# The compute engines of a two-layer transformer trunk, ordered by another scheduler model

## Chip, cores, metric

One core of one Trainium2 chip. The metric is device microseconds of one launch, the median of several runs.

## What is computed

Two layers over 512 tokens of width 1024: 256 context tokens, which read only each other, and 256 latent tokens, which read all. Each layer takes one normalised and modulated input through three token mixers (latent attention, "MLA"; differential attention; windowed attention with a sink), merges them with gates, projects, and then runs a SwiGLU feed-forward. A small product with `w_ada` gives each layer its shifts, scales and gates.

```python
def merge_branches(o_a, o_b, o_c, gates, wa, wb, wc, wo):
    ga, gb, gc = jnp.split(gates, N_BRANCH, axis=-1)
    return (ga * (o_a @ wa) + gb * (o_b @ wb) + gc * (o_c @ wc)) @ wo
...
def swiglu(h, w_gate_up, w_down):
    g, u = jnp.split(h @ w_gate_up, 2, axis=-1)
    return (jax.nn.silu(g) * u) @ w_down
...
def adaln(cond, w, b):
    return jnp.split(jax.nn.silu(cond) @ w + b, 6, axis=-1)
```

## The kernel before

**Tiling.** The tokens stand in four tiles of 128. Every product of two matrices is made in three passes on numbers that are split into a high and a low part (`mm3`, L267, L268, L269: high by high, high by low, low by high). A weight block is loaded by SyncE into one of three `raw` buffers (`do_load`, L166); ScalarE casts the high part into one of three `hl` buffers (L139) and VectorE subtracts to get the low part (L140). The load of a later block can go out only when a `raw` buffer has been split.

**Attention** runs as steps S, E, T, V (`attend`). S is a product into `psS` (L721, L791). E finds the row maximum on VectorE (L663, with L665 and, for the window, a floor), takes the exponential on ScalarE (L667), and for every second step a reciprocal (L739, L800) and the scaling of the weights on VectorE (L745; L801, L803, L804 for the differential mixer). T transposes the weights on TensorE (L673), V multiplies by the values (L758). There are two `psS` buffers, so an S waits for the L667 of two steps earlier. L1059 and L1036 copy queries and values of the MLA into place; L823 sums squares of the differential output; L382 and L383 finish a gate.

**The ada stream** (`ada_dve`) is spread through the other work of a layer: two `aw` buffers, loaded by SyncE (L350), are multiplied and summed on VectorE by L401 and L403 (16 instructions for each half of a quarter), then TensorE sums over the partitions (L361), ScalarE copies (L363), TensorE transposes (L367). A gate goes by another way: its row is written to memory (L372) and read back to all partitions into `gw` (L380), L376 and L377 load what L382 and L383 add and multiply.

**Between the sub-layers** `normed` (L431 to L436), `modulate_T` (transposes L442; L455 on VectorE for one half and L457 on ScalarE for the other; L459 and L460 split the result into `hT`) and `residual` (sum of squares L298, L475, L477 and L479 on GpSimd, L482) make the next input from the last product.

**The order.** TensorE and SyncE run in the order in which the program is written, since the trunk declares these two engines to be ordered by hand:

```python
    ctx.enter_context(tc.manual_schedule(engines={mybir.EngineType.PE, mybir.EngineType.SP}))
```

The program interleaves attention steps, blocks of weights and the ada stream by a table of costs (`drive`, `fillers`, `attend`). The queues of VectorE, ScalarE and GpSimd are ordered at compile time by the scheduler of the tile framework, from the same program, by a model of when each instruction can run. Each engine then runs its queue in that order, and where the head of a queue waits, all behind it wait as well.

## Time and profile before

| | |
|---|---|
| median of 3 runs | 1530.48 us (1529.92 to 1534.97) |
| profiled execution | 1534.5 us |
| its span | 1532.7 us |
| TensorE, matmuls, busy | 1464.7 us, 96% |
| TensorE, weight loads, busy | 1228.9 us, 80% |
| VectorE busy | 1028.6 us, 67% |
| ScalarE busy | 690.0 us, 45% |
| GpSimd busy | 155.8 us, 10% |
| mean granted clock of TensorE | 0.986 |

The profiled execution took 4.0 us more than the median of the three. A share of busy time is a mean over stages; where TensorE waits and for whom is to be seen in the waits and on the time line. On this time line layer 0 has its MLA from 103 to 225 us, the differential mixer to 345, the window mixer to 482, the merge and output projection to 620, gate-up with the ada stream to 860, down to 985. Layer 1 has its mixers to 1260, the output projection to 1340, gate-up to 1466, and ends at 1532.

### The profile page before, as it was taken

To read this page: it belongs to the slowest core of one execution; us is meant where nothing else is said; L and a number is where in the kernel's file an instruction comes from. 1 tells how busy PE (TensorE), PEld (TensorE's weight loads), DVE (VectorE), ACT (ScalarE), POOL (GpSimd) and SP (SyncE) were. 2 spreads that over 40 slices of the span, in tenths; PEclk is the share of its full clock that TensorE was granted. 3 is DMA by queue.
4 is the path that set the end of the run, shared out by engine and by line. 5 is a ranking of instruction groups with operands and counts; after the bars stand their busy time and mean duration, and the time that the engine had idled before them with its cause. 6 is when DMAs were issued, how large, how long until landed. Compare 5 with 4: busy or idle time off the path is not lost. (4 is left out here: it accounts for less than half of the span.)

```text
span 1532.7 us, 23209 instructions
## 1 busy us (share of the span) xinstructions
PE 1464.7 (96%) x8827; PEld 1228.9 (80%) x8827; DVE 1028.6 (67%) x2035; ACT 690.0 (45%) x1293; POOL 155.8 (10%) x217
## 2 busy tenths in 40 slices
PE   6989999998999999999999999998999999999998
PEld 5866677876777879887777788886898899799986
DVE  4678766887885554687877323578677776666654
ACT  4565554444554345332232213565555564544443
POOL 1222100022110001000000000133101300100000
PEclk9989999999999999999999999999999999999999
DMA  9532223434332452566567334424436436667664
GB/s 288 154 106 69 69 83 97 110 84 137 95 98 72 144 170 83 163 194 176 168 192 219 110 97 128 148 79 135 108 93 155 130 99 190 195 194 218 207 219 166
DMA packets 254243, 216.25 MB, mean 141 GB/s; under 512 B 24426, under 2 KB 236084, under 8 KB 254132
## 3 DMA queue, kind: packets, MB, share of 16 engines
q1 hardware_dynamic: 252464, 209.98, 47.0%
q10 hardware_dynamic: 1668, 4.80, 0.8%
q8 instruction: 69, 1.13, 0.3%
q14 instruction: 42, 0.34, 0.1%
HBM read 209.48 MB, written 5.27 MB: 140 GB/s over the span
## 5 line engine op out<-in xcount | busy, mean ns | idle before, releaser
L267 PE MATMUL psg<-hT,hl 128*128 128x256 f32 (+1 forms) x1328 | 478.2, 360 | 0.0
L268 PE MATMUL psg<-hT,hl 128*128 128x256 f32 (+1 forms) x1328 | 451.4, 340 | 0.3 <-DVE hT L460 0.3
L269 PE MATMUL psg<-hT,hl 128*128 128x256 f32 (+1 forms) x1328 | 451.3, 340 | 0.1
L140 DVE TENSOR_TENSOR hl<-raw,hl 128x1024 fp32r<-128x1024 f32 (+2 forms) x243 | 293.4, 1209 | 201.0 <-ACT hl L139 200.1
L139 ACT CAST hl<-raw 128x1024 fp32r<-128x1024 f32 (+2 forms) x243 | 243.6, 1004 | 318.8 <-PE psg L269 185.7
L267 PEld LDWEIGHTS psg<-hT,hl 128*128 128x128 f32 x1328 | 254.2, 191 | 37.8 <-issue 14.4
L269 PEld LDWEIGHTS psg<-hT,hl 128*128 128x128 f32 x1328 | 253.7, 191 | 28.9 <-DVE hl L140 0.3
L268 PEld LDWEIGHTS psg<-hT,hl 128*128 128x128 f32 x1328 | 254.8, 192 | 25.3 <-issue 4.2
L403 DVE SCALAR_TENSOR_TENSOR acc<-aw,siluc,acc 128x256 f32<-128x256 f32 x448 | 201.7, 485 | 14.0 <-DMA aw<-in_w_ada 11.4
L667 ACT ACTIVATE work<-psS,nm 128x512 f32<-128x512 f32 (+1 forms) x96 | 59.1, 616 | 51.9 <-DVE nm L665 47.6
L477 POOL TENSOR_SCALAR smy<-ssy 128x1 f32<-128x1 f32 x12 | 4.1, 339 | 725.8 <-ACT work L298 725.8
L673 PE MATMUL psT<-ca,work 128*128 128x128 f32 x400 | 65.1, 278 | 8.3 <-DVE work L804 3.8
L663 DVE TENSOR_REDUCE nm<-psS 128x1 f32<-128x512 f32 (+1 forms) x96 | 57.1, 595 | 18.7 <-PE psS L721 11.4
L267 PE MATMUL psg<-oT,hl 128*128 128x512 f32 (+1 forms) x192 | 69.5, 362 | 0.0
L673 PEld LDWEIGHTS psT<-ca,work 128*128 128x128 f32 x400 | 48.6, 143 | 21.6 <-issue 8.5
L269 PE MATMUL psg<-oT,hl 128*128 128x512 f32 (+1 forms) x192 | 64.8, 338 | 0.2 <-DVE hl L140 0.2
L268 PE MATMUL psg<-oT,hl 128*128 128x512 f32 (+1 forms) x192 | 64.7, 337 | 0.0
L676 ACT COPY work<-psT 128x512 f32<-128x512 f32 (+1 forms) x72 | 36.8, 511 | 54.5 <-PE psT L673 54.2
L267 PE MATMUL psg<-hl,hT 128*128 128x256 f32 (+1 forms) x168 | 57.8, 344 | 2.7 <-ACT hT L139 2.7
L721 PE MATMUL psS<-kT,qT 96*128 96x512 f32 (+1 forms) x96 | 45.6, 560 | 10.6 <-ACT work L667 10.6
L269 PE MATMUL psg<-hl,hT 128*128 128x256 f32 (+1 forms) x168 | 48.1, 286 | 0.8 <-DVE hT L140 0.8
L268 PE MATMUL psg<-hl,hT 128*128 128x256 f32 (+1 forms) x168 | 47.7, 284 | 0.0
(325 smaller groups left out, 2572.2 us busy)
## 6 DMA issues: line engine op xcount, KB each, us to landing
raw<-in_w_gate_up SPq DMA_DIRECT2D x88, 512.0 KB
aw<-in_w_ada SPq DMA_DIRECT2D x80, 512.0 KB
raw<-in_w_in SPq DMA_DIRECT2D x78, 512.0 KB
raw<-in_w_down SPq DMA_DIRECT2D x44, 512.0 KB
aw<-in_w_ada SPq DMA_DIRECT2D x32, 256.0 KB
raw<-in_w_o SPq DMA_DIRECT2D x16, 512.0 KB
raw<-in_w_branch_a SPq DMA_DIRECT2D x8, 512.0 KB
raw<-in_w_in SPq DMA_DIRECT2D x16, 256.0 KB
```

The lines of the kernel that those rows point to most:

```text
L139: nc.scalar.copy(hi, src)
L140: nc.vector.tensor_tensor(lo, src, hi.bitcast(F32), ALU.subtract)
L267: nc.tensor.matmul(ps, lhsT=asl(a[0], k), rhs=bsl(b[0], k), start=st, stop=False)
L268: nc.tensor.matmul(ps, lhsT=asl(a[0], k), rhs=bsl(b[1], k), start=False, stop=False)
L269: nc.tensor.matmul(ps, lhsT=asl(a[1], k), rhs=bsl(b[0], k), start=False, stop=en)
L403: nc.vector.scalar_tensor_tensor(acc[:, s], w[:, k], sc, acc[:, s], ALU.mult, ALU.add)
L477: nc.gpsimd.tensor_scalar(sm, ss[:, 0:1], ss[:, 1:2], D * EPS, ALU.add, ALU.add)
L663: nc.vector.tensor_reduce(nm, ps[:, :nk], AX.X, ALU.max, negate=True)
L667: nc.scalar.activation(st["p"][:, :nk], ps[:, :nk], AF.Exp, bias=nm, accum_out=sm)
L673: nc.tensor.transpose(pt[:, k * P:(k + 1) * P], st["p"][:, k * P:(k + 1) * P], ident)
L676: nc.scalar.copy(st["pT"][:, :nk], pt[:, :nk])
L721: nc.tensor.matmul(st["ps"][:, :nk], lhsT=q, rhs=k, start=z == 0, stop=z == len(ops) - 1 and mk is None)
```

## The change

The context that holds the program gets one argument more, by which the compile-time scheduler uses its time-line model instead of its default model.

```diff
-    with tile.TileContext(nc) as tc:
+    with tile.TileContext(nc, schedule_with_timeline_sim=True) as tc:
         trunk(tc, *args)
```

Instructions are the same in number and kind. The queues of TensorE and SyncE are the same row by row, 7178 and 314 rows. VectorE's queue reads 1566 rows in place of 1555, ScalarE's 919 in place of 927; GpSimd's keeps its 198 rows, some in another order. 864 tiles lie in another buffer of their pool. In the MLA stage, the first L663 and L665 that stood behind four L1059 copies stand ahead of them; at about 169 us an L665 stands ahead of an L143 and of the L955 and L956 of a stack of operands, behind which it stood; and at about 123 us two L401 and two L403 stand ahead of an L745 where one L403 stood. In the window mixer, at about 413 us, six L403, one L663 and one split L140 stand between two L401 and an L745 that stood right behind them. Three other places, shown below:

VectorE, differential mixer of layer 0 (about 250 us), up to the scaled weights of one step, L804, for which its transposes wait. `hl` and `raw` are a weight block, `aw`, `siluc` and `acc` the ada stream, `nmd`, `sm` and `rsd` maximum, sum and reciprocal of the softmax. Before, from the reciprocal L800 on:

```order
L800 RECIPROCAL rsd<-sm_2613 128x2
L663 TENSOR_REDUCE nmd<-psS 128x1
L140 TENSOR_TENSOR hl<-raw,hl 128x1024
L801 TENSOR_TENSOR rsd<-rsd,lam 128x1
L403 SCALAR_TENSOR_TENSOR acc<-aw,siluc,acc 128x256
L803 TENSOR_SCALAR work<-work,rsd 128x256
L403 SCALAR_TENSOR_TENSOR acc<-aw,siluc,acc 128x256
L804 SCALAR_TENSOR_TENSOR work<-work,rsd 128x256
```

and after, from one L403 ahead of it:

```order
L403 SCALAR_TENSOR_TENSOR acc<-aw,siluc,acc 128x256
L800 RECIPROCAL rsd<-sm_2613 128x2
L403 SCALAR_TENSOR_TENSOR acc<-aw,siluc,acc 128x256
L663 TENSOR_REDUCE nmd<-psS 128x1
L140 TENSOR_TENSOR hl<-raw,hl 128x1024
L403 SCALAR_TENSOR_TENSOR acc<-aw,siluc,acc 128x256
L801 TENSOR_TENSOR rsd<-rsd,lam 128x1
L403 SCALAR_TENSOR_TENSOR acc<-aw,siluc,acc 128x256 x2
L803 TENSOR_SCALAR work<-work,rsd 128x256
L823 TENSOR_REDUCE ssd<-work 128x4
L663 TENSOR_REDUCE nmd<-psS 128x1
L804 SCALAR_TENSOR_TENSOR work<-work,rsd 128x256
```

Five L403 in place of two, the sum of squares L823 and one more maximum L663 now stand ahead of L804; just ahead of this piece three L403 stand in place of two.

VectorE, gate-up of layer 0 (about 662 us). `gw` is the gate that a DMA brings back, `raw` the weight block to split. Before:

```order
L140 TENSOR_TENSOR hl<-raw,hl 128x1024
L140 TENSOR_TENSOR aT<-work,aT 128x512
L403 SCALAR_TENSOR_TENSOR acc<-aw,siluc,acc 128x256
L140 TENSOR_TENSOR hl<-raw,hl 128x1024
L382 TENSOR_TENSOR gw<-gw,work 128x256 x2
L383 SCALAR_TENSOR_TENSOR gw<-gw,work 128x256 x2
L401 TENSOR_SCALAR acc<-aw,siluc 128x256 x2
```

and after:

```order
L403 SCALAR_TENSOR_TENSOR acc<-aw,siluc,acc 128x256
L140 TENSOR_TENSOR hl<-raw,hl 128x1024
L140 TENSOR_TENSOR aT<-work,aT 128x512
L382 TENSOR_TENSOR gw<-gw,work 128x256 x2
L140 TENSOR_TENSOR hl<-raw,hl 128x1024
L383 SCALAR_TENSOR_TENSOR gw<-gw,work 128x256 x2
L401 TENSOR_SCALAR acc<-aw,siluc 128x256 x2
```

The second split of a weight block (L140 `hl`) has moved behind the two L382, which read `gw`.

ScalarE, end of layer 0 (about 985 us), where the last tiles are normalised and the first weights of layer 1 are cast:

```order
+L139 CAST hl<-raw 128x1024
 L436 ACTIVATE work<-xt,rn 128x512
-L457 ACTIVATE work<-psS,mod_6997,mod_6555 128x128 x5
-L459 CAST hT<-work 128x4x128 x2
-L457 ACTIVATE work<-psS,mod_6997,mod_6555 128x128 x3
+L457 ACTIVATE work<-psS,mod_6997,mod_6555 128x128 x8
 L298 ACTIVATE work,ssy<-psV 128x512
-L459 CAST hT<-work 128x4x128
-L139 CAST hl<-raw 128x1024
+L459 CAST hT<-work 128x4x128 x3
```

The cast of a weight block (L139) has moved to the front, the eight L457 run together, and the sum of squares L298 of the last product stands ahead of all three L459, of which two stood ahead of it.

On VectorE at the same point, two L460, which follow those L459, have moved behind L140 `hl`, two L475, another L460 and two L482.

At about 1331 us the VectorE split L140 `hl` stands ahead of the second L482, behind which it stood.

## Rows read from the trace of the kernel before

**Rows 1.** The page, part 1: busy us, share of the span and instructions of each engine.
```profile
PE 1464.7 (96%) x8827; PEld 1228.9 (80%) x8827; DVE 1028.6 (67%) x2035; ACT 690.0 (45%) x1293; POOL 155.8 (10%) x217
```

**Rows 2.** Waits of TensorE over the span: us in total, times, longest us.
```profile
PE psS L721 <- ACT work L667: 16.0, 10, 2.6
```

**Rows 3.** Waits of VectorE over the span, same columns.
```profile
DVE acc L401 <- DMA aw<-in_w_ada: 30.4, 21, 5.0
DVE gw L382 <- DMA gw<-row: 27.7, 14, 4.6
```

**Rows 4.** Two stretches: length, busy us of PE, PEld, DVE, ACT, POOL, granted clock, DMA.
```profile
121.00:126.00 5.00, 4.24 (x11) 2.85 (x12) 4.46 (x13) 2.49 (x7) 0.00 (x0) 0.66 0.34 106
711.00:717.00 6.00, 5.24 (x21) 4.00 (x22) 4.99 (x12) 1.81 (x3) 0.00 (x0) 0.72 0.59 179
```

**Rows 5.** Time line of TensorE, eight places: start, duration, operation, [idle before, releaser].
```profile
121.76 1.44 PE L721 MATMUL psS<-kT,qT 96*128 96x512 f32 x2 [2.35 <-ACT work L667]
...
169.86 0.90 PE L721 MATMUL psS<-kT,qT 96*128 96x256 f32 x2 [2.22 <-ACT work L667]
...
255.04 0.41 PE L673 MATMUL psT<-ca,work 128*128 128x128 f32 x2 [1.21 <-DVE work L804]
...
415.94 0.60 PE L673 MATMUL psT<-ca,work 128*128 128x128 f32 x4
...
711.76 0.42 PE L361 MATMUL psT<-acc,ones 128*32 128x128 f32 x6 [1.66 <-DVE acc L403]
...
989.07 0.40 PE L267 MATMUL psg<-kept,hT 128*128 128x288 f32 x1 [0.74 <-ACT hT L459]
...
989.79 0.40 PE L269 MATMUL psg<-kept,hT 128*128 128x288 f32 x1 [0.20 <-DVE hT L460]
...
1334.46 0.66 PE L442 MATMUL psT<-ca,work 128*128 128x128 f32 x4 [0.93 <-DVE work L435]
```

**Rows 6.** Time line of VectorE in the MLA stage of layer 0.
```profile
118.42 1.19 DVE L1059 COPY qT<-work 32x256 f32<-32x256 f32 x4 [0.63 <-POOL work L639]
119.62 0.69 DVE L663 TENSOR_REDUCE nm<-psS 128x1 f32<-128x512 f32 x1
```

**Rows 7.** Time line of VectorE in the differential and the window stage of layer 0.
```profile
254.82 0.67 DVE L823 TENSOR_REDUCE ssd<-work 128x4 f32<-128x512 f32 x1
...
412.94 0.35 DVE L401 TENSOR_SCALAR acc<-aw,siluc 128x256 f32<-128x256 f32 x1 [1.29 <-DMA aw<-in_w_ada]
...
413.53 0.48 DVE L745 TENSOR_SCALAR work<-work,rsd 128x512 f32<-128x512 f32 x1
```

**Rows 8.** Time line of VectorE in the gate-up stage of layer 0.
```profile
662.75 1.22 DVE L140 TENSOR_TENSOR hl<-raw,hl 128x1024 fp32r<-128x1024 f32 x1
668.20 0.76 DVE L382 TENSOR_TENSOR gw<-gw,work 128x256 f32<-128x256 f32 x2 [4.23 <-DMA gw<-row]
...
674.90 3.25 DVE L403 SCALAR_TENSOR_TENSOR acc<-aw,siluc,acc 128x256 f32<-128x256 f32 x8
```

**Rows 9.** Time line of SyncE's queue there: issues of DMAs.
```profile
664.00 0.37 SPq L166 DMA_DIRECT2D raw<-in_w_gate_up  x1
664.41 1.96 SPq L350 DMA_DIRECT2D aw<-in_w_ada  x1
```

**Rows 10.** Time line of ScalarE at the end of layer 0.
```profile
986.05 0.72 ACT L436 ACTIVATE work<-xt,rn 128x512 f32<-128x512 f32 x1 [1.07 <-POOL rn L433]
986.67 1.83 ACT L457 ACTIVATE work<-psS,mod,mod 128x128 f32<-128x128 f32 x5
988.39 1.15 ACT L459 CAST hT<-work 128x512 fp32r<-128x512 f32 x2
...
990.45 0.63 ACT L298 ACTIVATE work<-psV 128x512 bf16<-128x512 f32 x1
```

**Rows 11.** Time line of VectorE in layer 1, behind the output projection.
```profile
1331.86 1.22 DVE L140 TENSOR_TENSOR hl<-raw,hl 128x1024 fp32r<-128x1024 f32 x1
1333.92 0.48 DVE L435 TENSOR_SCALAR work<-xt,rn 128x512 f32<-128x512 f32 x1 [0.84 <-POOL rn L433]
```

## The prediction

> **What bounds the kernel now.** I read the busy shares first. TensorE multiplies for 96% of the span, VectorE works for 67% of it, ScalarE for 45% [rows 1]. So the time is TensorE's own work plus 68 us (1532.7 minus 1464.7) in which it has nothing to run, and a change of order on other engines can only move those gaps and the clock. It can't touch the 1464.7 us, except where a gap lowers the clock. The waits come next. TensorE's largest is for score buffers: `psS` L721 waits ten times, 16.0 us, for the exponential L667 [rows 2], which itself waits for a row maximum on VectorE. VectorE in turn waits for DMAs of the ada stream: 30.4 us for weights and 27.7 us for gate rows [rows 3]. Since each queue runs in its compiled order, those waits hold whatever stands behind them. Then the clock: after a wait of 2.35 us TensorE ran at a mean granted 0.66 over 5 us, after one of 1.66 us at 0.72 over 6 us [rows 4, 5]. That mixes its two levels, 1.2 and 2.4 GHz, and costs 5.0 x 0.34 = 1.7 us and 6.0 x 0.28 = 1.7 us. So a long wait has a tail of about 1.7 us. Last I read the time lines at places where TensorE waits in the trace of before. At such a place there is no slack: whatever the awaited instruction loses is lost by TensorE.
>
> The order of TensorE and SyncE stays, so I went along VectorE's and ScalarE's new queues and asked, at each place, how much work has come ahead of the instruction that TensorE waits for.
>
> **MLA of layer 0, a gain: -4 us.** Before, four copies L1059 waited for GpSimd and ran from 118.42 to 119.62; the maximum L663 came behind them [rows 6], the exponential behind that, and TensorE waited 2.35 us [rows 5]. Now L663 and L665 stand ahead of the copies, so this wait goes, with its tail of 1.7 us. The wait of 2.22 us at 169.86 [rows 5] has the same kind, and the order moves the L665 forward there too. Together 2.35 + 2.22 + 2 x 1.7 = 8.0 us. Against it, the scales L745, for which the transposes L673 wait, get more L401 and L403 ahead of them in the same stage. One L403 costs 3.25 / 8 = 0.40 us of the queue [rows 8]. At the place that the part on the change names, two L401 (priced as L403) and one L403 more are 1.2 us. I take three such places and some 0.1 us of new waits on top, 4 us, half of the gain. Net -4; bounds -8 (nothing lost) and +2 (a tail of 1.7 us comes back at two of the three places as well).
>
> **Differential mixer: +5 us.** At 255.04 TensorE waited 1.21 us for L804 [rows 5]. Ahead of L804 there now stand four more L403 (1.6 us), the sum of squares L823 (0.67 us [rows 7]) and one more L663, half as wide as the one of 0.69 us [rows 6] and so about 0.35 us. That is 2.6 us with nothing to hide it. What comes early here is missing later, so not each of the sixteen L804 (four heads by four tiles) pays; I take two such places, 5 us. Bounds: one place (2.6) and three with a tail (9.5).
>
> **Window mixer: +4 us.** At 413 us the two L401 wait for a DMA until 412.94, and L745 followed at 413.53 [rows 7]. Now six L403 (2.4 us), an L663 (0.69 us) and a split L140 (1.22 us, as in [rows 8]) come between, 4.3 us. The transposes that need it start at 415.94 without a wait [rows 5], and L745 was done by 414.01, so 1.9 us are covered and 2.4 us are not. One further place at four L403 makes 4. Bounds 2.4 and 9, the upper end for three places at 2.4 and a tail.
>
> **Gate-up of layer 0: +8 us.** This is the largest term and the least sure. L382 waited 4.23 us, until 668.20, for the gate's row [rows 8]. The split of a weight block ran just before that wait, at 662.75, and has now moved behind both L382. It starts at about 668.20 + 0.7 = 668.9, 6.1 us later. SyncE's next load of `raw` went out at 664.00, when this split had freed the buffer, and the next load of the ada stream stands behind it, at 664.41 [rows 9]. Both go 6.1 us later, the second at about 670.5. Its data are multiplied from about 674.90 on [rows 8]. Before there were 10.5 us between issue and use, now some 5.6 (the split has moved VectorE's own work back by 1.2). Nothing shows the landing time, so the bounds are 0 (it lands in 5.6 us) and 6.1 (all of it goes into the stream). I take 6.1, because the stream waits for `aw` so often [rows 3] that it looks paced by its loads, and at 711.76 TensorE waits for that stream without slack [rows 5]. With one more tail of 1.7 us, 8. Downwards the bound is 0; upwards 15, if a second gate quarter pays 6.1 again.
>
> **End of layer 0: +4 us.** TensorE waited 0.74 us at 989.07 for the first of two L459 [rows 5], which began at 988.39 [rows 10]. Ahead of it now stand three more L457 (1.83 / 5 = 0.37 us each, 1.1) and the L298 (0.63 us): it begins 1.7 us later. The weight cast that has moved to the front falls into the 1.07 us in which ScalarE waited for GpSimd at 986.05 [rows 10], and costs nothing if its block has landed by then. If it hasn't, it delays everything. The L460 on VectorE, for which TensorE waited 0.20 us at 989.79 [rows 5], have moved behind L482, and that waits for GpSimd, and this for L298. I put this at another 2.3 us. Bounds 1.7 and 8.
>
> **Output projection of layer 1: +2 us.** A split of 1.22 us has moved ahead of the second L482 [rows 11], from which L435 follows, and TensorE waits 0.93 us for L435 at 1334.46 [rows 5]. So 1.2 us, and some for the L460 behind it. Bounds 1 and 5.
>
> **Mixers of layer 1 and the rest: 0.** One wait on `psS` goes and several fills come ahead of scales. Bounds -4 and +4. GpSimd's few moves wait for the same producers as before.
>
> **Sum.** -4 + 5 + 4 + 8 + 4 + 2 = +19 us on the profiled execution's 1534.5, that is 1553.5. That execution stood 4.0 us above the median, so the forecast for the median is 1549.5, taken as 1550.
>
> **Rivals.**
> *The score waits decide (faster).* The new order puts maxima ahead of copies and fills. If it does so everywhere, up to the whole 16.0 us of [rows 2] goes, with two tails (3.4). If the late aw load of the gate-up lands in time, the losses outside attention are 6 us, and the scales give back some 5: 19.4 - 11 = 8 us faster, 1522. For it: this is TensorE's largest wait. Against: 255.04 and 415.94 show losses in attention of the same size. It decides if landing takes less than 5.6 us and at most two scales fall late.
>
> *Order is hidden by idle time (same).* VectorE idles a third of the span [rows 1], and the fills that come early leave room later. Then gains and losses are both near 4 and the median stays at 1530. Against it stand the waits without slack.
>
> The busy shares alone would put TensorE first and make this rival likely. The Trainium skill, in "Perfetto Trace Analysis", section "Identifying the Most-Contended Engine", says that the engine with the highest occupancy is the one to work on, and that matmul busy share is a poor measure for TensorE. By that rule a new order on engines at 67% and 45% would be worth nothing; the waits in rows 2 and 5 speak against reading it so here.
>
> *The gate wait is paid at every quarter (much slower).* If VectorE never makes up the lag in gate-up, 6.1 us come three times more: 1550 + 18 = 1568. For it: fourteen L382 waits [rows 3]. Against: the order shows the split behind L382 at one quarter of this gate, not at all.
>
> That the new argument does nothing is excluded, since the queues differ.
>
> **Chances.** Forecast 0.53, much slower 0.20, same 0.13, faster 0.14. A measurement of this kernel can tell about 0.3% (4.6 us) from no change. So faster 0.14, same 0.13, slower 0.73. The range runs from 1526, inside the faster rival, to 1574, above the dearest; a tenth is left out at either end.
>
> **What would show it.** In the changed profile, the `psS` wait on L667 should fall below 12 us, with the one near 121.76 gone. The transposes L673 should wait longer for L804 and L745, together by 8 us or so. TensorE's first new wait in gate-up should stand at or before the L361 that was at 711.76 and be some 6 us long, and ScalarE's L459 should come late at the end of layer 0. I'm wrong if gate-up takes its 240 us as before, or if the waits for the scales don't grow.

## The result: 2.4% slower

| | before | after |
|---|---|---|
| median | 1530.20 us (4 runs, 1529.57 to 1534.97) | 1569.78 us (4 runs, 1562.09 to 1570.44) |
| profiled execution's span | 1532.7 us | 1567.9 us |
| mean granted clock of TensorE | 0.986 | 0.979 |

The ratio is 1.0238, with a 95% interval of 1.0210 to 1.0267. The forecast was 1550 with a range of 1526 to 1574. The sign was right and the time lies inside the range, but the sum, +19 us, was half of the +39.6 us measured (by the interval of the ratio, 32 to 41).

The page of after, part 1, answers to [rows 1]:

```profile
PE 1472.7 (94%) x8827; PEld 1235.7 (79%) x8827; DVE 1032.5 (66%) x2035; ACT 691.2 (44%) x1293; POOL 148.8 (9%) x217
```

TensorE was busy for 8.0 us more with the same instructions, which goes with its lower clock. The other 27.2 us of the span are idle time. Its three largest waits, and VectorE's for the ada stream and the gates, answer to [rows 2, 3] (us in total, times, longest):

```profile
PE psT L673 <- DVE work L745: 18.4, 11, 3.0
PE psT L673 <- DVE work L804: 9.6, 6, 3.8
PE psS L721 <- ACT work L667: 7.5, 5, 2.8
```

```profile
DVE acc L401 <- DMA aw<-in_w_ada: 46.7, 31, 4.4
DVE gw L382 <- DMA gw<-row: 35.4, 15, 5.8
DVE acc L403 <- DMA aw<-in_w_ada: 26.0, 17, 3.6
```

In the kernel before, three of these were:

```profile
PE psT L673 <- DVE work L804: 3.8, 5, 1.7
...
PE psT L673 <- DVE work L745: 2.2, 3, 0.9
```

```profile
DVE acc L403 <- DMA aw<-in_w_ada: 11.4, 9, 2.2
```

The score waits were halved, from 16.0 to 7.5 us. The waits of the transposes for the scales L745 and L804 grew from 2.2 and 3.8 us to 18.4 and 9.6. VectorE's waits for the ada weights grew from 41.8 us (30.4 at L401, 11.4 at L403) to 72.7.

TensorE's queue is the same in both kernels, so its 8827 matmuls can be lined up one by one. The difference of their start times is the lag, and a step in it marks the place that lost or gained. Two places in the changed kernel, on VectorE and then TensorE:

```profile
250.78 1.28 DVE L403 SCALAR_TENSOR_TENSOR acc<-aw,siluc,acc 128x256 f32<-128x256 f32 x3 [2.49 <-DMA aw<-in_w_ada]
...
257.14 0.67 DVE L823 TENSOR_REDUCE ssd<-work 128x4 f32<-128x512 f32 x1
257.74 0.40 DVE L663 TENSOR_REDUCE nmd<-psS 128x1 f32<-128x256 f32 x1
258.07 0.47 DVE L804 SCALAR_TENSOR_TENSOR work<-work,rsd 128x256 f32<-128x256 f32 x1
...
422.93 0.62 DVE L401 TENSOR_SCALAR acc<-aw,siluc 128x256 f32<-128x256 f32 x2 [3.00 <-DMA aw<-in_w_ada]
...
428.35 0.47 DVE L745 TENSOR_SCALAR work<-work,rsd 128x512 f32<-128x512 f32 x1
```

```profile
258.68 0.50 PE L673 MATMUL psT<-ca,work 128*128 128x128 f32 x2 [3.75 <-DVE work L804]
...
428.96 0.63 PE L673 MATMUL psT<-ca,work 128*128 128x128 f32 x4 [2.84 <-DVE work L745]
```

The first is the wait of 1.21 us at 255.04 in [rows 5], now 3.75; the lag behind that execution steps by 2.54 there, where the prediction had 2.6. In the kernel before, the L403 ahead of this place had waited too:

```profile
249.53 0.88 DVE L403 SCALAR_TENSOR_TENSOR acc<-aw,siluc,acc 128x256 f32<-128x256 f32 x2 [1.87 <-DMA aw<-in_w_ada]
```

The second had no wait before. VectorE sat idle for 3.00 us at an L401 (1.29 in [rows 7]), with the scale behind it in its queue.

A single execution is a weak ruler for the total: 15 runs of the kernel before lie between 1528.82 and 1536.92 us, and its profiled execution and that of a kernel that differs from it in one row are 6.5 us apart, mostly in the attention stages. So totals are told as medians. The lag of a whole stage is read against the execution that stood nearer to its median, that of the one-row kernel below (span 1526.2 us); where the other one gives something else, both are told. Steps of the lag are placed by the times of the kernel before.

### The profile page after: what moved, and what is told of

Its sections match the earlier page's. It is cut to its first block, busy times and chain, and to the rows that moved or that the text cites. A ratio compares the mean times of both kernels' runs of the same rounds, so it can differ in the third digit from the quotient of the medians.

```text
span 1567.9 us, 23217 instructions
## 1 busy us (share of the span) xinstructions
PE 1472.7 (94%) x8827; PEld 1235.7 (79%) x8827; DVE 1032.5 (66%) x2035; ACT 691.2 (44%) x1293; POOL 148.8 (9%) x217
## 5 line engine op out<-in xcount | busy, mean ns | idle before, releaser
L140 DVE TENSOR_TENSOR hl<-raw,hl 128x1024 fp32r<-128x1024 f32 (+2 forms) x243 | 292.2, 1204 | 190.8 <-ACT hl L139 189.7
L139 ACT CAST hl<-raw 128x1024 fp32r<-128x1024 f32 (+2 forms) x243 | 242.9, 1004 | 315.2 <-PE psg L269 192.2
L403 DVE SCALAR_TENSOR_TENSOR acc<-aw,siluc,acc 128x256 f32<-128x256 f32 x448 | 203.4, 492 | 28.3 <-DMA aw<-in_w_ada 26.0
L673 PE MATMUL psT<-ca,work 128*128 128x128 f32 x400 | 65.2, 278 | 30.9 <-DVE work L745 18.4
L663 DVE TENSOR_REDUCE nm<-psS 128x1 f32<-128x512 f32 (+1 forms) x96 | 57.1, 595 | 20.9 <-PE psS L721 14.4
L267 PE MATMUL psg<-hl,hT 128*128 128x256 f32 (+1 forms) x168 | 58.0, 345 | 1.7 <-ACT hT L139 1.7
L401 DVE TENSOR_SCALAR acc<-aw,siluc 128x256 f32<-128x256 f32 x64 | 21.0, 358 | 46.7 <-DMA aw<-in_w_ada 46.7
L140 DVE TENSOR_TENSOR kept<-raw,kept 128x1024 fp32r<-128x1024 f32 (+2 forms) x26 | 31.0, 1194 | 28.3 <-ACT kept L139 28.1
L269 PE MATMUL psg<-hl,hT 128*128 128x256 f32 (+1 forms) x168 | 48.4, 288 | 0.4 <-DVE hT L140 0.4
```

The lines of the kernel that those rows point to most:

```text
L139: nc.scalar.copy(hi, src)
L140: nc.vector.tensor_tensor(lo, src, hi.bitcast(F32), ALU.subtract)
L267: nc.tensor.matmul(ps, lhsT=asl(a[0], k), rhs=bsl(b[0], k), start=st, stop=False)
L269: nc.tensor.matmul(ps, lhsT=asl(a[1], k), rhs=bsl(b[0], k), start=False, stop=en)
L401: nc.vector.tensor_scalar(acc[:, s], w[:, k], sc, None, ALU.mult)
L403: nc.vector.scalar_tensor_tensor(acc[:, s], w[:, k], sc, acc[:, s], ALU.mult, ALU.add)
```

## Experiments

**How an order was held.** After the program is traced, a function adds an edge between neighbours of a queue. It orders them and adds no wait. Instructions below number 900, about the first 90 us, are left to the scheduler. Held in the order of the kernel before, VectorE and ScalarE run the same instructions row by row in the trace (the run with the default order held, below), and the one-row kernel below, held in this way, takes the time of the kernel before.

```diff
+def pin(tc, nc, queues):
...
+    for engine, order in queues:
+        ins = [i for i in nc.cur_bb.bb.instructions if i.engine == engine]
+        ins.sort(key=lambda i: int(i.name.split("-")[1]))
...
+        q = [ins[k] for k in order]
+        for a, b in zip(q, q[1:]):
+            if min(int(a.name[2:]), int(b.name[2:])) < FIRST:
+                continue
+            tc.add_manual_dep(b, a.name, mybir.DependencyInfo(mybir.DependencyClass.NoSync, mybir.DependencyReason.DATA), reason="pin")
...
         trunk(tc, *args)
+        pin(tc, nc, QUEUES)
```

`QUEUES` has the three orders. In the stage runs, it is the order of before, in which the instructions of one stretch of time stand in the order of after.

### One stage in the changed order, all else as before

**Attention of layer 0, 100 to 482 us.**

> The three engines' queues are as before, except that what ran between 100 and 482 us stands in the changed order. Local theory: the loss is the sum of single places, and a stage keeps its loss when it stands alone. Lining up the two traces matmul by matmul, TensorE's lag grew by -0.5 us in the MLA stage, by 6.3 in the differential and by 8.1 in the window mixer, so the span should grow by 14 us (1546 to 1548), nearly all of it at about 255, 312, 377, 416 and 457 us, and not at all behind 482. Rival (spread): the loss comes from buffers that moved all over the program, or from an ada stream that runs late as a whole; then this stage alone gives under half of it, below 7 us. The prediction's own terms for these stages (-4, +5, +4) give +5.

1547.12 us (2 runs) against 1530.33, ratio 1.0107 (1.0076 to 1.0138): +16.8 us. Lined up, MLA gained 2.4 us, the differential mixer lost 9.4 and the window mixer 10.3 (against the profiled execution of the kernel before: 4.7, 7.9 and 7.7). Nothing came back behind 482. The local theory holds, the spread one falls, and the prediction's +5 was too small.

**Gate-up of layer 0, 620 to 860 us.**

> The three engines' queues are as before, except that what ran between 620 and 860 us stands in the changed order. Local theory: the lag in this stage grew by 9.1 us in the changed kernel, so the span grows by 8 to 10 us here. Rival: the stage was late there because it came in with a stream that was already late; alone it gives under 3 us. The prediction's term was +8, from the one split moved behind the gate wait at 668 us.

1538.93 us, ratio 1.0069 (1.0042 to 1.0097): +8.6 us by the medians, 6.6 on the lag. The size is the prediction's. The place isn't, as the next run shows.

**The one row on which the prediction put this.** `L140 hl` goes behind the two `L382`:

```diff
 L403 SCALAR_TENSOR_TENSOR acc<-aw,siluc,acc 128x256
-L140 TENSOR_TENSOR hl<-raw,hl 128x1024
 L382 TENSOR_TENSOR gw<-gw,work 128x256 x2
+L140 TENSOR_TENSOR hl<-raw,hl 128x1024
```

> One row of VectorE's queue is moved: the split L140 that ran at 662.75 us goes behind the two L382 that wait for the gate's row; all else as before. The prediction's step: the next weights of the ada stream are issued about 6 us later and the stream takes the whole delay, +6.1 us and a tail of 1.7, to be seen at the L361 at 711.76. Rival: in the changed kernel that issue was 6.2 us later, but L403 then waited only 0.77 us for the weights, so the delay is hidden in the 10 us between issue and use; then this row costs 1 us or less.

1530.09 us, ratio 0.9993 (0.9978 to 1.0008): nothing. VectorE, SyncE's queue and TensorE in this kernel:

```profile
660.38 0.76 DVE L382 TENSOR_TENSOR gw<-gw,work 128x256 f32<-128x256 f32 x2 [5.51 <-DMA gw<-row]
661.06 1.22 DVE L140 TENSOR_TENSOR hl<-raw,hl 128x1024 fp32r<-128x1024 f32 x1
...
668.25 3.25 DVE L403 SCALAR_TENSOR_TENSOR acc<-aw,siluc,acc 128x256 f32<-128x256 f32 x8
```

```profile
662.30 0.37 SPq L166 DMA_DIRECT2D raw<-in_w_gate_up  x1
662.72 0.57 SPq L350 DMA_DIRECT2D aw<-in_w_ada  x1
```

```profile
705.16 0.42 PE L361 MATMUL psT<-acc,ones 128*32 128x128 f32 x6 [1.66 <-DVE acc L403]
```

The load goes out behind the late split, as predicted, but the eight L403 that use it (a half of a quarter is eight of these instructions here, not 16) start 5.5 us after its issue without a wait. TensorE's wait at L361 is 1.66 us, as in [rows 5]. The prediction had named this bound (lands in 5.6 us, cost 0) and taken the other.

**The end of layer 0, 980 to 1003 us,** and then ScalarE's part of it alone.

> The three engines' queues are as before, except that what ran between 980 and 1003 us stands in the changed order. Local theory: TensorE's waits at 989.07 and 989.79 grew by 4.1 and 1.3 us in the changed kernel, so +5 us, less what comes back by 1012 (0.7), that is 4 to 6. The prediction's term was +4, of which 1.7 on ScalarE. Rival: part of it was inherited from a late weight load that only the changed gate-up and down stages made; then 2 us or less.

> As before, except that ScalarE's queue between 980 and 1003 us stands in the changed order; VectorE's stays as before. The prediction's step for ScalarE: three more L457 and one L298 ahead of the first L459, 1.7 us, to be seen at 989.07. If the moved weight cast also waits for its block, 3.8 to 4 us as when all engines have the changed order. If the loss needs VectorE's moves, under 1 us.

All engines: 1536.37 us, ratio 1.0045 (1.0029 to 1.0062), +6.0. ScalarE alone: 1535.11, ratio 1.0026 (1.0014 to 1.0037), +4.9 by the medians and +3.8 on the lag at the first wait. ScalarE alone, and TensorE:

```profile
986.08 1.05 ACT L139 CAST hl<-raw 128x1024 fp32r<-128x1024 f32 x1 [1.76 <-DMA raw<-in_w_in]
987.04 0.71 ACT L436 ACTIVATE work<-xt,rn 128x512 f32<-128x512 f32 x1
987.66 2.88 ACT L457 ACTIVATE work<-psS,mod,mod 128x128 f32<-128x128 f32 x8
```

```profile
992.20 0.61 PE L267 MATMUL psg<-kept,hT 128*128 128x288 f32 x1 [4.53 <-ACT hT L459]
```

The cast at the head of ScalarE's queue waits for its weight block. The wait at L459, 0.74 us in [rows 5], is 4.53 here. So most of this loss is ScalarE's, about half of it a DMA wait that the prediction had hoped would be over. With all engines in the changed order the L460 on VectorE adds 1.3 us at 989.79.

**The second half of gate-up, 760 to 860 us.**

> As before, except that what ran between 760 and 860 us stands in the changed order. The only kind of move there: a split L140 that stood ahead of the L401 of the next ada half stands behind it. That split frees the buffer for which SyncE's next weight load waits, and the next ada load stands behind that load, so the stream waits for itself. Theory: the whole loss of the gate-up stage alone (6.5 us on the time line) is made here, in waits of TensorE at about 814, 821 and 846, 5 to 7 us. Rival: the first half of the stage matters (moves at 640 to 720), and this gives under 2.

1533.19 us, ratio 1.0029 (1.0015 to 1.0042): +2.9 by the medians, 4.6 on the lag. That is short of the theory's 5 to 7 and above the rival's 2. The largest step, 2.6 us, is at one place:

```profile
800.44 0.35 DVE L401 TENSOR_SCALAR acc<-aw,siluc 128x256 f32<-128x256 f32 x1 [1.94 <-DMA aw<-in_w_ada]
800.71 1.22 DVE L140 TENSOR_TENSOR hl<-raw,hl 128x1024 fp32r<-128x1024 f32 x1
```

```profile
801.96 0.37 SPq L166 DMA_DIRECT2D raw<-in_w_gate_up  x1
802.37 1.86 SPq L350 DMA_DIRECT2D aw<-in_w_ada  x2
```

```profile
811.58 0.63 PE L361 MATMUL psT<-acc,ones 128*32 128x128 f32 x4 [2.56 <-DVE acc L403]
```

The split stands behind an L401 that waits for ada weights. SyncE's next `raw` load waits for the split, and the next `aw` load stands behind that. So the stream delays its own next load, and the wait for it at the L403 grows: 1.55, 2.24, 2.31 and 3.32 us at 765.92, 777.86, 789.19 and 807.43. The first half adds one place: with all of gate-up in the changed order, TensorE waits 2.14 us at 704.15 for a split, L140, that stands behind fills and behind an L401 that waited 1.27 us. The wait of 1.66 us at the next L361 goes with it. In the changed kernel itself that place has no step; there the lag grew by 0.9 us up to 760 and by 8.3 up to 860.

**The end of the output projection of layer 1, 1320 to 1345 us.**

> The three engines' queues are as before, except that what ran between 1320 and 1345 us stands in the changed order: on VectorE a split L140 ahead of the second L482, and one L401 (which waited 1.45 us for its weights) and two L403 ahead of the two L460. The prediction's term: +2, of which 1.2 for the split, seen at 1334.46, and the rest guessed for L460. Local theory from the two traces: 1.0 at 1334.46 and 2.2 at 1337.96, and up to 5 in the stage as a whole, since the L460 wait behind an L401 that waits for its weights. Rival: only the split counts; about 1 us.

1537.30 us, ratio 1.0039 (1.0023 to 1.0055): +5.6 us.

```profile
1337.48 0.35 DVE L401 TENSOR_SCALAR acc<-aw,siluc 128x256 f32<-128x256 f32 x1 [2.19 <-DMA aw<-in_w_ada]
1337.87 1.00 DVE L403 SCALAR_TENSOR_TENSOR acc<-aw,siluc,acc 128x256 f32<-128x256 f32 x2
1338.79 0.68 DVE L460 TENSOR_TENSOR hT<-work,hT 128x512 fp32r<-128x512 f32 x1
```

```profile
1333.23 0.66 PE L442 MATMUL psT<-ca,work 128*128 128x128 f32 x4 [1.92 <-DVE work L435]
...
1339.53 0.58 PE L268 MATMUL psg<-hT,hl 128*128 128x256 f32 x1 [2.72 <-DVE hT L460]
```

The split ahead of L482 costs 1.0 (0.93 to 1.92), as predicted. The L460 behind a waiting L401 costs 2.4 more.

The four stages alone give 16.8 + 8.6 + 6.0 + 5.6 = 37.0 of 39.6 us by the medians (by the ratios, 2.6% of the time against 2.4%); the four intervals together allow some 7 us either way. Within that, the loss is local and adds up. What the 864 tiles in other buffers do by themselves was not run.

### Is it the fills' work or the waits that they carry?

The ada stream was given a third weight buffer and loads two halves ahead. The buffers have the tag `xt`, which the tiles `xt` of the activations use too; these were set to three buffers with it (two lines more), in all runs of this part:

```diff
-            w = sp.tile([P, 4, 256], F32, tag="xt", bufs=2, name="aw")
+            w = sp.tile([P, 4, 256], F32, tag="xt", bufs=3, name="aw")
...
-        nxt = raw(0, 0)
+        halves = [(i, h) for i in range(len(todo)) for h in range(2)]
+        nxt = [raw(*halves[0]), raw(*halves[1])]
...
-                w = nxt
-                if h == 0 or i + 1 < len(todo):
-                    nxt = raw(i + h, 1 - h)
+                w = nxt.pop(0)
+                if 2 * i + h + 2 < len(halves):
+                    nxt.append(raw(*halves[2 * i + h + 2]))
```

In these kernels the numbers of the lines from 387 on are higher by one, so that L402 and L404 are the fills, L746 and L805 the scales. First with each model free to make its own order:

> Default order, but the ada stream has three weight buffers instead of two and loads two halves ahead instead of one. VectorE then should hardly wait for ada weights: those waits were 41.8 us in the kernel before (30.4 at L401, 11.4 at L403) and should fall below 15. Of the few places where these waits reach TensorE in the default order (711, 744, 846 us), 4 to 6 us should come back, so about 1525. Theory that only the fills' own time matters: no change within 0.3%.

> The time-line order, with the same three buffers. In the changed kernel VectorE waited 72.7 us for ada weights (46.7 at L401, 26.0 at L403), 31 us more than before, and scales and splits stood behind those waits. Theory of held queues: the waits are what makes awaited work late, so with the loads early most of the loss goes, and the excess over the default order with three buffers falls from 39 us to 20 or less. Theory of filled queues: the fills' own 0.40 us each, put ahead of the scales, are the loss; then the excess stays above 30.

Default: 1519.28 us, ratio 0.9931 (0.9911 to 0.9951), a larger gain than the 1525 expected. Time-line: 1568.22, ratio 1.0238 (1.0210 to 1.0267), no better than with two buffers. This went against the theory of held queues, until VectorE's waits were read. In the time-line kernel:

```profile
DVE acc L404 <- DMA aw<-in_w_ada: 47.2, 28, 4.6
...
DVE acc L402 <- DMA aw<-in_w_ada: 21.6, 12, 4.9
```

They were still there, 68.8 us, against 22.0 us (11.7 and 10.3; under 15 was expected) in the default kernel. With the third buffer in the program, the model's new order left VectorE waiting all the same. So the two theories weren't told apart, and the order had to be held still.

> Three ada buffers, with the queues of VectorE, ScalarE and GpSimd held in the order that the default model gave for two buffers (the kernel before's). It is the partner of the run with the time-line order held. Theory that the loads themselves are worth something: 1516 to 1524, as with the default model's own order for three buffers. If that gain came from the new order and not from the loads: 1528 or more.

> Three ada buffers as in the two runs before, but the three engines' queues are held in the order that the time-line model gave for two buffers (the changed kernel's; the first 90 us, which the pins leave, in the default order). In the run where the model saw the third buffer it put the fills earlier, and VectorE still waited 68.8 us for ada weights. Here the order can't follow. Theory of held queues: those waits fall below 25 us and the excess over the default order with three buffers (about 1519) falls to 20 or less, so 1540 or below; the waits of TensorE for L745 and L804, 28 us in the changed kernel, fall below 14. Theory of filled queues: the fills' own time ahead of the scales and splits is the loss; the waits for weights fall all the same, but the time stays above 1550.

| three buffers, order made for two | median | ratio to before |
|---|---|---|
| default order held | 1516.78 us | 0.9908 (0.9879 to 0.9938) |
| time-line order held | 1531.39 us | 1.0006 (0.9990 to 1.0021) |

VectorE in the held time-line order:

```profile
DVE acc L402 <- DMA aw<-in_w_ada: 6.6, 3, 4.4
DVE acc L404 <- DMA aw<-in_w_ada: 1.9, 1, 1.9
```

TensorE there:

```profile
PE psT L674 <- DVE work L746: 11.4, 9, 3.3
PE psT L674 <- DVE work L805: 5.7, 5, 3.1
```

With the waits gone (72.7 to 8.5 us; the partner has 8.4), the excess of the time-line order over its partner falls from 39.6 to 14.6 us, below the 20 that the theory of held queues allowed. The waits for the two scales came to 17.1, not below 14. So some 25 us of the loss go with the late ada loads, and some 15 are what else stands ahead of awaited work. Each of the two excesses is known to some 5 us, and a little of the 25 belongs to the first 90 us, which aren't held (the lag of the changed kernel at 100 us was 1.5).

By stage the two shares differ. Lined up with its partner, the held time-line order loses 1.9 us in gate-up (the changed kernel 9.2 against the one-row kernel), 4.8 in the window mixer (10.8) and 6.0 in the differential mixer (7.7; 6.3 against the kernel before), and gains 3.8 in MLA (a loss of 1.8, or a gain of 0.6). These are single executions, but the differences are clear in gate-up: its loss is nearly all late loads, the window mixer's about half. The differential mixer's is hardly any: VectorE waited there for ada weights for 11.6 us before and for 6.9 in the changed kernel. In the held run it has no such wait in that stage, and the two steps at L804 are still there, 1.6 and 2.5 us. What is left there is the work put ahead of L804, and the clock. At the end of layer 0, the cast starts at 974.29 without a wait in the held run, and TensorE's step at ScalarE's `hT` is 2.1 us, near the 1.7 that the prediction had for the three L457 and the L298.

### A kernel that beats both

> Three ada buffers and the default order of the kernel before, except that what ran at 118 to 124, 140 to 150, 158 to 190 and 1045 to 1058 us stands in the changed order: the places where the changed kernel took waits of psS L721 away (2.8, 1.1, 2.4, 1.1 and 2.3 us between the lined-up traces). If these gains are local they add to those of the loads: 6 to 9 us below the partner without them, 1510 to 1515. If the places that lose in the same stage take it back, no better than the partner.

1506.80 us, ratio 0.9843 (0.9819 to 0.9867). It is 10.0 us below its partner by the medians, more than the 6 to 9 expected (5.7 between the two profiled executions), and 23.7 below the kernel before. Lined up, the gain over the partner is 7.6 us in MLA of layer 0; the steps at the score waits are 1.9, 1.1, 2.4, 1.1 and, in layer 1, 2.2 us, the steps at places that lose are between 0.7 and 1.7. The time-line model's orders are good at these places.

## Why the prediction was right in sign and short in size

**That the waits without slack decide** was right. Busy shares would have made "same" likely, and the trace had already spoken against reading them so. The ten score waits fell, as forecast below 12 us, and the losses at the scales were larger.

**MLA, -4:** -2.4 in the run of the attention stage; in the changed kernel -0.6 or +1.8, according to the execution that it is lined up with. The mechanism stands: the waits at 121.76 and 169.86 went, and scales took most of the gain back (1.1 to 2.0 us at four places). The size can't be told from that scatter. The upper bound of +2 doesn't follow from its own words: -4 and two tails of 1.7 are -0.6.

**Differential, +5:** 9.4, or 6.3 in the changed kernel against the kernel before. The count of two places was right, and so was the first: 2.6 forecast and 2.5 seen at 255.04; the second, at 311.97, is 1.4 to 1.7. The step that failed is the tail, which this term had only in its upper bound. In the attention run TensorE was granted 0.50 from 251.3 to 258.1 us, behind the first wait, and from 312.8 to 316.2, behind the second; the lag grew by 2.8 and 1.3 us there. In the changed kernel 258 to 263 us ran at a granted 0.66 after the wait of 3.75 us.

**Window, +4:** 10.3. The first place was right: 2.4 forecast and 3.0 seen at 415.94. The step that failed is the count, "one further place". Steps of the lag stand at 375, 377, 416 and 457 (1.0, 2.1, 3.0 and 2.0 us), the first of them at a score wait, a kind of wait of which the prediction had counted only the gains.

**Gate-up, +8:** 8.6 by the median, 6.6 on the lag, but the step behind the term is wrong. The split behind the gate wait costs nothing: its load came in time. The sign given for it, a new wait of some 6 us at or before the L361 at 711.76, didn't come; the changed kernel gained 1.9 us at that L361. What costs is a split behind fills or behind a waiting L401, 40 and 140 us later. That the sum came out right is luck, from a wrong place; without the other places the term would have been 0, the lower bound given.

**End of layer 0, +4:** 6.0. The three L457 and the L298 were priced well. The cast was put at nothing "if its block has landed by then", and it had not, by 2.09 us in the changed kernel; where it had, in the held run with three buffers, the whole step was 2.1 us. VectorE's L460 behind L482, to which the prediction gave 2.3, cost 1.3.

**Output projection, +2:** 5.6. The split was priced well, the L401 that waits for its weights ahead of L460 was left as "some".

**Mixers of layer 1, 0:** the lag changed by -0.4 to -1.0 us there, inside the bounds.

In the window mixer, at the end of layer 0 and behind the output projection the same was left out. I priced an instruction that moved ahead by its own time, 0.40 us for a fill, and not by the wait that it takes to the head of the queue. [Rows 3] had 30.4 of the 41.8 us of those waits, and [rows 7] show one of them. The held orders put that share at some 25 of 39.6 us, and gate-up, where the sum was right by luck, has the largest part of it. The differential mixer isn't of this kind: pricing its fills by their own time was right.

**The rivals.** The faster one is half true: 8.5 us of score waits went, and the combined kernel has that gain with few of the losses. The "much slower" one lay nearest to the measured time, 1568, but its mechanism, the gate wait paid at every quarter, was not what happened: the gate row costs nothing even once.

## What to carry to other kernels

An instruction that moves ahead in an engine's queue takes its wait along. Price it by the time at which its operand lands, above all when a DMA brings it; its duration alone is the price only where the operand has landed. In the differential mixer here the duration was the larger part; in gate-up it was the wait. A scheduler's model may be chosen stage by stage: hold the better order of each, line the traces up on the engine whose order is fixed, and keep the places that gain. When an operand is late, loading it a step earlier helps only an order that doesn't move with it.

## What was not expected of the hardware and the tools around it

The time-line model's own order for three buffers left VectorE as much waiting as for two (68.8 and 72.7 us), while the order that it had made for two waited 8.5 with the same early loads. That its model has a load land sooner than the chip does would explain this; no run shows the model's own landing times, so it stays open.

A kernel whose queues are the kernel before's but for one row had a profiled span of 1526.2 us, and the kernel before 1532.7, with medians that agree (1530.09 and 1530.33). In the MLA stage the mean granted clock was 0.96 and 0.94. So single executions of nearly one order differ by 6 us, as much as most of the terms here.
